# The first gates of a late block copied on the chip, and attention's background steps set by their count, in a hybrid decoder block

## The chip, the cores and the metric

The kernel runs on one core of a Trainium2 chip. The core has TensorE for matmuls (PE in the profile; PEld is its weight load), VectorE (DVE), ScalarE (ACT), GpSimd (POOL) and SyncE (SP). Each executes its own instructions in order, and they meet by semaphores. DMA transfers are issued here by SyncE (plain ones) and by GpSimd (gathers by a list of indices). The metric is the device time of one execution in microseconds (us), less is better.

## What is computed

The reference is one decoder layer on 1024 tokens of width 1024, in float32:

```python
h = rmsnorm(x, norm1_g) * (1 + sc1) + sh1
mq, mk, mv, mo, mi, mf, dq, dk, dv = split(h @ w_in)       # 4 mLSTM heads, 4 attention heads
hm = rmsnorm(mlstm_chunkwise(silu(conv(mq, mk)), mv, gates(mi, mf))) * sigmoid(mo)
od = rmsnorm(softmax(q1 k1) v - lam * softmax(q2 k2) v) * (1 - lam_init)   # causal, 2 maps a head
x = x + g1 * (concat(hm, od) @ w_out)
h2 = rmsnorm(x, norm2_g) * (1 + sc2) + sh2
x = x + g2 * peer(h2)
out = rmsnorm(x, final_g)
```

`peer` takes for each token and each of 8 heads the 16 best of 16384 experts (product keys, 128 x 128), so 128 experts a token. With gate g (a softmax over the 16) and expert rows u, v of length 1024 it sums g * gelu(h2 . u) * v.

## The kernel before, in words

The tokens are eight blocks of 128. They pass the **front** in three groups (`GROUPS`, 2, 3 and 3 blocks): `front_T` (norm and transpose), `front_proj` (seven projections, whose weights stream in 256 KB pieces `wr` through seven buffers on SyncE's queue), `front_mix` (what is left of attention and mLSTM, and their norms), `front_out`, `front_norm2` and `front_keys` (queries, keys, the search for the best experts).

The experts of blocks 0, 1, 6 and 7 are **gathered**: for each of the 128 places one gather of rows u (`gu`, 512 KB) that VectorE multiplies with h2, then one of rows v (`gv` or `gvr`) that is summed into `ga`. The experts of blocks 2 to 5 (`DENSE`) go by **dense** matmuls over all 16384 experts: for each of 128 keys j, `s_mm` makes `ge` = gelu(h2 . u), `s_gate` multiplies it by the gates `Gt` and splits it into W (two parts), and `v_step` multiplies W by the rows v into `ps_dA`. `s_mm` runs up to 14 keys ahead (`AHEAD`).

The gates of a dense block are made by `gates`: 32 steps, each of two VectorE operations (`oh`), eight matmuls (`ps_g`) and one ScalarE copy into `stg`. Four steps fill one `stg` (1 MB: all 128 keys of 16 tokens), which is then written to `G_d` in DRAM (32 writes for the four blocks). `load_G(j)` reads the gates of eight keys from there for all tokens (2 MB) into the one buffer `Gt`. Blocks 2 to 4 are handled in the front as a background stream (`all_gates`). Block 5 is the **late** block: it comes with the third group, and its gates are made inside `dense`, with buffers of `LateMem`, while the first `s_mm` run. So the first `Gt` is read in two loads: 1.5 MB for the three early blocks, and, when all late steps are through, 512 KB for the late one.

Work that runs beside the projections is kept in `background` as generators with a rate. `tick` adds the rate to each one's account and advances it once per whole unit. `proj_T` and `proj_R` call `tick` behind each piece of weights, `att_S` calls it for each part of scores, and `front_mix` between attention's steps. The rates: the gathers 1.6 (`RG`), the tables of gates 1.5 (`RP`), mLSTM 0.4 and 1.0, attention `AR[k]`. `attention` yields once for the first unit's scores and twice for each unit, a unit being one head of one block; `att_load` reads a head's `akT` and `avh` from DRAM. When the projections are over, `front_mix` takes the remaining streams of its group off the list and runs them out itself:

```python
k = 0
for _ in o.att[0]:
    k += 1
    if k % 2 or k % 4 == 0:
        next(steps, None)
        tick()
for _ in steps:
    pass
```

All this writes a program order. A planner then orders the instructions of every engine by that order (shifted by priorities: the late steps ahead, the gathers that are left over after the front behind it, and `dense` behind those) and by its own costs; the engines execute the result as it stands.

Of the kernel before, what the change touches and what calls it, by code (L numbers as in the profile page):

```python
# [15 lines left out]
AF = mybir.ActivationFunctionType  # L16
# [5 lines left out]
P = 128  # L22
# [6 lines left out]
HD = 4  # L29
# [22 lines left out]
def kernel(ctx: ExitStack, tc: tile.TileContext, x, c_col, ada_w, ada_b, ada_bc, n1c,  # L52
                             w_in, conv_w, conv_b, gate_b, mngc, lq1, lk1, lq2, lk2, dngc, w_out,
                             n2c, n2r, wq, skT, pu, puT, pv, fg, out, dbg=None):
    nc = tc.nc
# [4 lines left out]
    LPACE = ()  # L60
    PJ = 0
    ALT = 1
    AR = [0.6, 0.5, 0.3]
    SOG = [8, 0, 8]
    DEF = 0
    N1G = 2
# [28 lines left out]
    J, JG = 4, 8  # L95
# [233 lines left out]
    TS = 16  # L329
# [362 lines left out]
    def front_proj(o):  # L692

        n, nb, t0 = o.n, o.nb, o.t0
# [9 lines left out]
        nc.sync.dma_start(vd_d[t0 * P:t0 * P + n, :].rearrange("(b p) e -> p b e", p=P), vst[:, :nb])  # L704
        o.a_, o.b_ = mlstm_rows(o.hT, nb)
        o.mix = [fr.tile([P, D], F32, tag="rows", name="mix", bufs=RB) for _ in range(nb)]
        o.att = [attention(o), AR[o.k], 0.0]
        background.append(o.att)
        overlapped.append(o)
        o.qk = []  # L710
# [34 lines left out]
    def attention(o):  # L745

        units, o.ams = att_heads(o.t0, o.nb, o.dq, o.mix)
        att_S(units[0])
        yield
        for k, u in enumerate(units):  # L750
            if k + 1 < len(units):
                att_S(units[k + 1])
            yield
            att_T(u)
            att_V(u)
            yield
# [443 lines left out]
            nc.sync.dma_start(quarter(out, c), xo[c * 32:(c + 1) * 32])  # L1200

    class FrontMem:
        gs = staticmethod(lambda s, d: fr.tile(s, d, tag="gs", name="gs", bufs=1))
        gh = staticmethod(lambda s, d: fr.tile(s, d, tag="gh", name="gh", bufs=1))
        dT = staticmethod(lambda s, d: fr.tile(s, d, tag="dT", name="dT", bufs=DB))
        stg = staticmethod(lambda s, d: fr.tile(s, d, tag="stg", name="stg", bufs=SB))
# [4 lines left out]
    def gates(ii, gf, db, wide, mem=None):  # L1211
# [5 lines left out]
        mem = mem or FrontMem()  # L1217
# [20 lines left out]
        def close(oh, stg, tg, q):  # L1238
            pg = mem.bank("ps_g")
            for r in range(4):  # L1240
                for i in range(np_):
                    nc.tensor.matmul(pg[:, r * P:(r + 1) * P], oh[:, 0, :, r], oh[:, 2 + i, :, r],  # L1242
                                     start=i == 0, stop=i == np_ - 1)
            nc.scalar.activation(stg[:, :, q * 4:q * 4 + 4].rearrange("p j t -> p t j"),  # L1244
                                 pg.rearrange("p (t j) -> p t j", t=4), AF.Copy)
            if q == TS // 4 - 1:
                nc.sync.dma_start(G_d[db * (P // TS) + tg], stg)

        for tg in range(P // TS):
            stg = mem.stg([P, P, TS], F32)  # L1250
# [12 lines left out]
    @contextmanager  # L1263
    def later(offset):

        tc.cur_priority += offset
        yield
        tc.cur_priority -= offset


    def dense(d1, d2, d3, d4, psS, psA):
        n = NDB * P
        blocks = DENSE + MIXED
        na = len(blocks) * P
# [3 lines left out]
        Gt = {}  # L1278
        d1.tile([P, 72], F32, name="pad")

        def load_G(j, parts=((0, na // TS),)):
            if parts[0][0] == 0:
                Gt[0] = d1.tile([P, na // TS, JG, TS], F32, tag="G", name="Gt", bufs=GD)
            for lo, hi in parts:
                nc.sync.dma_start(Gt[0][:, lo:hi], G_d[lo:hi, :, j:j + JG, :].rearrange("a p j t -> p a j t"))

        class LateMem:
# [2 lines left out]
            gh = staticmethod(lambda s, d: d4.tile(s, d, tag="gh", name="gh", bufs=1))  # L1290
            dT = staticmethod(lambda s, d: d4.tile(s, d, tag="dT", name="dT", bufs=1))
            halves = []

            @staticmethod
            def stg(s, d):
# [10 lines left out]
        if gating:  # L1306
            early = gating[0][2] * P // TS
            load_G(0, ((0, early),))
            late = (s for g in gating for s in gates(*g, mem=LateMem))
        else:  # L1310
            load_G(0)
            acc = d4.tile([P, len(blocks), D], F32, tag="dacc", name="dacc", bufs=1)
# [115 lines left out]
        if gating:  # L1428
            with later(-LP):
                for _ in late:  # L1430
                    pass
            load_G(0, ((early, na // TS),))
            acc = d4.tile([P, len(blocks), D], F32, tag="dacc", name="dacc", bufs=1)
        for j in range(J):
            s_gate(j)
# [129 lines left out]
```

## Time and profile before

| what | us |
|---|---|
| median of 3 runs | 2989.22 |
| lowest and highest run | 2983.14, 2993.66 |
| the profiled execution | 2983.2 |
| its span in the profile | 2981.3 |
| TensorE busy | 2783.4 |
| VectorE busy | 2382.0 |
| GpSimd busy | 1282.8 |
| ScalarE busy | 973.6 |

The profile shows one execution. Its span runs from the first instruction to the last. "Busy" is the time in which an engine executed matmuls or other compute; the clock is the share of full speed that was granted to TensorE. A row of a group shows the count, the summed busy time in us, the mean of one in ns, and, behind the second bar, the idle time of the engine just ahead of these instructions with what ended it. `<-` reads "written from" or "waits for".

### The profile page before, as it was taken

Reading aid. Unit: us, or ns where it says so; the run is one execution under the profiler, and the core shown is the slowest. Engines: PE = TensorE matmul, PEld = TensorE weight load, DVE = VectorE, ACT = ScalarE, POOL = GpSimd, SP = SyncE. Lnnn points to the kernel's source line nnn. Section 1 sums busy time; section 2 is a strip of 40 time slices with the busy share of each in tenths; the row PEclk is TensorE's granted clock in tenths of the full one; section 3 lists DMA queues with packets and bytes.
Section 4 is the critical chain, followed back from the end, with each engine's and each line's share of the span. In section 5 each row is a group of like instructions: output and inputs, shape, how many; then the busy total and the mean of one; then the engine's idle time right before and its main releaser. Section 6 shows DMA issues by size and latency. Waiting matters only on the chain.

```text
span 2981.3 us, 40087 instructions
## 1 busy us (share of the span) xinstructions
PE 2783.4 (93%) x13686; PEld 2076.9 (70%) x13686; DVE 2382.0 (80%) x5489; ACT 973.6 (33%) x1695; POOL 1282.8 (43%) x1083
## 2 busy tenths in 40 slices
PE   6899999689999997999995999999999999999998
PEld 5547757465556765766574878878777788877786
DVE  5634999856997687357977988889988889988876
ACT  1432344312235445232453322322322323322232
POOL 0000266654555453334654555545554444544400
PEclk9989999689999999999997999999999999999999
DMA  8745699999998888998788999999899999999962
GB/s 280 252 138 180 209 360 336 324 350 339 325 345 306 305 299 293 350 332 293 280 309 284 337 335 334 332 340 340 313 339 322 331 341 324 338 323 317 318 230 70
DMA packets 396848, 900.00 MB, mean 302 GB/s; under 512 B 34770, under 2 KB 184274, under 8 KB 392548
## 3 DMA queue, kind: packets, MB, share of 16 engines
q0 software_dynamic: 147456, 536.94, 50.1%
q1 hardware_dynamic: 249188, 360.51, 35.9%
q8 instruction: 108, 1.77, 0.2%
q14 instruction: 96, 0.79, 0.1%
HBM read 846.97 MB, written 50.35 MB: 301 GB/s over the span
## 4 chain that ended last, share of the span: by engine, by line
PE 50%; DVE 18%; DMA 13%; issue 11%; POOL 5%; ACT 2%; SPq 0%; DVEq 0%; POOLq 0%; ACTq 0%
PE ps_pj L403 11%; PE ps_dS L1338 9%; PE ps_dA L1370 9%; DMA Gt<-G_d 8%; PE ps_pj L423 7%; DVE gu L1028 4%; PE ps_g L1242 3%; PE ga L1090 3%; POOL gvr L1057 3%; DVE ga L1064 2%; DMA gu<-in_peer_u_dram,ei 2%; PE ps_S L605 2%; DVE dvs L1364 1%; DMA gv<-in_peer_v_dram,eT 1%; PE ps_tr L379 1%
## 5 line engine op out<-in xcount | busy, mean ns | idle before, releaser
L1024 POOL DMA_INDIRECT gu<-in_peer_u_dram,ei x512 | 657.3, 1284 | 928.6 <-DVE sv L912 347.9
L1370 PE MATMUL ps_dA<-dvs,W 128*128 128x512 f32 x2976 | 720.8, 396 | 56.9 <-ACT W L1348 27.4
L1338 PE MATMUL ps_dS<-dhT,us 128*128 128x512 f32 x3072 | 731.0, 391 | 1.2 <-POOL us L1331 1.2
L1370 PEld LDWEIGHTS ps_dA<-dvs,W 128*128 128x128 f32 x2976 | 566.1, 191 | 188.9 <-ACT W L1348 27.4
L1028 DVE SCALAR_TENSOR_TENSOR gu<-gu,h2r 128x1024 f32<-128x1024 f32 x512 | 620.1, 1222 | 72.3 <-DMA gu<-in_peer_u_dram,ei 59.1
L1338 PEld LDWEIGHTS ps_dS<-dhT,us 128*128 128x128 f32 x3072 | 576.2, 188 | 129.4 <-issue 8.0
L1057 POOL DMA_INDIRECT gvr<-in_peer_v_dram,ei x256 | 301.5, 1178 | 339.0 <-DVE ga L1064 184.4
L1076 POOL DMA_INDIRECT gv<-in_peer_v_dram,eT x256 | 275.8, 1077 | 266.0 <-PE ga L1090 148.2
L1064 DVE SCALAR_TENSOR_TENSOR ga<-gvr,w,ga 128x1024 f32<-128x1024 f32 x254 | 326.9, 1287 | 1.7 <-issue 0.3
L1363 ACT ACTIVATE dvs<-dv 128x512 fp32r<-128x512 f32 x248 | 155.7, 628 | 368.4 <-PE ps_dA L1370 164.5
L403 PE MATMUL ps_pj<-hT,wr 128*128 128x384 f32 (+1 forms) x768 | 233.7, 459 | 3.1 <-ACT ae L598 2.9
L403 PE MATMUL ps_pj<-h2T,wr 128*128 128x384 f32 (+1 forms) x768 | 231.2, 454 | 0.0
L1339 ACT ACTIVATE ge<-ps_dS 128x512 f32<-128x512 f32 x128 | 76.5, 598 | 424.4 <-PE ps_dS L1338 413.3
L1244 ACT ACTIVATE stg<-ps_g 128x512 f32<-128x512 f32 x128 | 134.0, 1064 | 238.0 <-PE ps_g L1242 164.1
L403 PEld LDWEIGHTS ps_pj<-hT,wr 128*128 128x128 f32 x768 | 144.9, 193 | 79.5 <-issue 9.8
L1255 DVE TENSOR_TENSOR oh<-iotah,dT 128x1024 f16<-128x1024 f16 x128 | 102.2, 804 | 118.5 <-PE ps_g L1242 94.7
L403 PEld LDWEIGHTS ps_pj<-h2T,wr 128*128 128x128 f32 x768 | 142.2, 190 | 73.3 <-issue 9.9
L423 PE MATMUL ps_pj<-wr,hT 128*128 128x256 f32 (+1 forms) x672 | 182.1, 425 | 3.5 <-DMA wr<-in_w_in_dram 2.7
L1364 DVE TENSOR_TENSOR dvs<-dv,dvs 128x512 fp32r<-128x512 f32 x248 | 171.9, 698 | 16.4 <-ACT dvs L1363 16.4
L1347 DVE SCALAR_TENSOR_TENSOR ge<-ge,Gt 128x512 f32<-128x512 f32 x128 | 87.3, 692 | 119.1 <-DMA Gt<-G_d 112.9
L423 PEld LDWEIGHTS ps_pj<-wr,hT 128*128 128x128 f32 x672 | 128.5, 197 | 45.4 <-issue 23.8
L1377 DVE TENSOR_TENSOR dacc<-dacc,ps_dA 128x512 f32<-128x512 f32 x240 | 156.1, 683 | 4.6 <-PE ps_dA L1370 4.6
(294 smaller groups left out, 3333.1 us busy)
## 6 DMA issues: line engine op xcount, KB each, us to landing
u<-in_peer_uT_dram SPq DMA_DIRECT2D x128, 512.0 KB
dv<-in_peer_v_dram SPq DMA_DIRECT2D x248, 256.0 KB
wr<-in_w_in_dram SPq DMA_DIRECT2D x168, 256.0 KB
G_d<-stg SPq DMA_DIRECT2D x32, 1024.0 KB
Gt<-G_d SPq DMA_DIRECT2D x15, 2048.0 KB
wmod<-in_ada_w_dram SPq DMA_DIRECT2D x48, 512.0 KB
wr<-in_peer_w_query_dram SPq DMA_DIRECT2D x96, 256.0 KB
wr<-in_w_out_dram SPq DMA_DIRECT2D x48, 256.0 KB
```

The lines of the kernel that those rows point to most:

```text
L403: nc.tensor.matmul(out[f], w2[:, kh, f * P:(f + 1) * P], hT[:, kb, :n], start=kb == 0 and f % k == 0, stop=kb == NC - 1 and f % k == k - 1)
L423: nc.tensor.matmul(out[f], hT[:, kb, f * P:(f + 1) * P], wk[:, kh], start=kb == 0 and f % k == 0, stop=kb == NC - 1 and (f % k == k - 1 or ...
L1024: nc.gpsimd.indirect_dma_start(out=u, out_offset=None, in_=pu, in_offset=bass.IndirectOffsetOnAxis(ap=o.ei[:, k:k + 1], axis=0))
L1028: nc.vector.scalar_tensor_tensor(u, u, 1.0, o.h2, op0=OP.mult, op1=OP.mult, accum_out=o.z[:, k:k + 1])
L1057: nc.gpsimd.indirect_dma_start(out=vt, out_offset=None, in_=pv, in_offset=bass.IndirectOffsetOnAxis(ap=o.ei[:, k:k + 1], axis=0))
L1064: nc.vector.scalar_tensor_tensor(o.acc, vt, o.w[:, k:k + 1], o.acc, op0=OP.mult, op1=OP.add)
L1076: got = nc.gpsimd.indirect_dma_start(out=vt, out_offset=None, in_=pv, in_offset=bass.IndirectOffsetOnAxis(ap=o.eT[:, t:t + 1], axis=0))
L1338: nc.tensor.matmul(ps, us[:, a, c], hT[:, b, c, sl], start=c == 0 and i == 0, stop=c == NC - 1 and i == 2)
L1363: nc.scalar.activation(vs[:, 0], v, AF.Copy)
L1364: nc.vector.tensor_sub(vs[:, 1], v, vs[:, 0])
L1370: nc.tensor.matmul(pacc[tb], w[:, a, tb * P:(tb + 1) * P], vs[:, b], start=jj == 0 and i == 0, stop=jj == J - 1 and i == 2)
L1377: nc.vector.tensor_add(o, o, pacc[tb])
```

## The change

Two edits. In `gates`, the first eight keys of each late `stg` are copied by ScalarE into `Gt` right after the `stg` is issued for writing, and the 512 KB load of the late block's first gates is dropped; the write to `G_d` stays, for the other keys. And attention's rate is no longer taken from the list 0.6, 0.5, 0.3: it is the number of attention's steps over the 32 ticks that follow in the projections, that is 17/32 = 0.53 for two blocks and 25/32 = 0.78 for three.

```diff
-    AR = [0.6, 0.5, 0.3]
...
-        o.att = [attention(o), AR[o.k], 0.0]
+        o.att = [attention(o), (2 * HD * nb + 1) / 32.0, 0.0]
...
     class FrontMem:
+        first = None
...
             if q == TS // 4 - 1:
                 nc.sync.dma_start(G_d[db * (P // TS) + tg], stg)
+                if mem.first is not None:
+                    nc.scalar.activation(mem.first[:, db * (P // TS) + tg], stg[:, 0:JG], AF.Copy)
...
             halves = []
+            first = None
...
             load_G(0, ((0, early),))
+            LateMem.first = Gt[0]
             late = (s for g in gating for s in gates(*g, mem=LateMem))
...
                 for _ in late:
                     pass
-            load_G(0, ((early, na // TS),))
             acc = d4.tile([P, len(blocks), D], F32, tag="dacc", name="dacc", bufs=1)
```

## Rows read from the trace of the kernel before

**Rows 1.** The page: the span, and the gate products of the dense part.

```profile
span 2981.3 us, 40087 instructions
...
L1347 DVE SCALAR_TENSOR_TENSOR ge<-ge,Gt 128x512 f32<-128x512 f32 x128 | 87.3, 692 | 119.1 <-DMA Gt<-G_d 112.9
```

**Rows 2.** Stretches: busy us (instructions) of PE, PEld, DVE, ACT, POOL; clock, DMA share, GB/s.

```profile
196.70:209.50 12.80, 6.28 (x49) 5.42 (x47) 7.21 (x37) 7.25 (x22) 0.00 (x0) 0.91 0.46 156
387.00:536.00 149.00, 141.99 (x610) 98.94 (x609) 137.81 (x327) 68.20 (x157) 104.54 (x77) 0.95 0.96 343
536.00:598.50 62.50, 31.85 (x101) 18.74 (x99) 54.38 (x141) 19.36 (x55) 38.35 (x31) 0.57 0.93 322
853.00:1068.00 215.00, 212.32 (x1278) 146.33 (x1277) 165.84 (x375) 99.29 (x184) 113.60 (x91) 0.97 0.89 310
1068.00:1183.40 115.40, 92.88 (x648) 59.26 (x647) 93.60 (x221) 59.23 (x129) 49.96 (x43) 0.93 0.87 312
1188.00:1484.00 296.00, 287.13 (x1942) 191.41 (x1939) 197.60 (x796) 97.45 (x130) 138.57 (x119) 0.99 0.90 318
...
1583.30:1610.70 27.40, 0.05 (x2) 0.01 (x1) 15.70 (x27) 2.40 (x5) 14.06 (x12) 0.50 0.94 340
1610.70:2846.00 1235.30, 1207.89 (x5222) 989.30 (x5223) 1113.10 (x1524) 369.76 (x556) 613.46 (x494) 0.99 0.94 328
```

**Rows 3.** Waits, 1575 to 1660: waiter, releaser, us, times, longest.

```profile
PE ps_dA L1370 <- ACT W L1348: 27.4, 1, 27.4
```

**Rows 4.** The chain that ended last: start us, us, what.

```profile
1591.69 17.57 DMA Gt<-G_d
...
1614.22 12.56 DMA Gt<-G_d
...
1841.64 5.44 PE ps_dS L1338 x24
```

**Rows 5.** Timeline of ScalarE, 1579 to 1616: start us, us, what.

```profile
1581.10 1.06 ACT L1244 ACTIVATE stg<-ps_g 128x512 f32<-128x512 f32 x1
...
1610.01 3.64 ACT L1348 ACTIVATE W<-ge 128x512 fp32r<-128x512 f32 x6 [24.97 <-DVE ge L1347]
```

**Rows 6.** Timeline of ScalarE, 568 to 612.

```profile
600.65 0.28 ACT L1051 ACTIVATE wT<-ga 128x128 f32<-128x128 f32 x1 [2.88 <-DVE eT L1049]
```

**Rows 7.** Groups by line, TensorE, 536 to 598.5.

```profile
L605 PE MATMUL ps_S<-akT,dq 64*128 64x512 f32 (+2 forms) x24 | 15.1, 754 | 7.8 <-DMA akT<-kd_d 7.8
L638 PE MATMUL ps_o<-avh,aT 128*128 128x128 f32 x46 | 10.8, 401 | 2.9 <-ACT aT L631 2.3 <-issue 0.6
L629 PE MATMUL ps_at<-ident,ae 128*128 128x128 f32 x21 | 5.1, 395 | 16.0 <-DVE ae L618 16.0
```

**Rows 8.** Groups by line, VectorE, 536 to 598.5.

```profile
L1028 DVE SCALAR_TENSOR_TENSOR gu<-gu,h2r 128x1024 f32<-128x1024 f32 x33 | 39.6, 1219 | 5.2 <-DMA gu<-in_peer_u_dram,ei 3.5 <-issue 1.7
```

**Rows 9.** Groups by line, TensorE, 1068 to 1183.4.

```profile
L605 PE MATMUL ps_S<-akT,dq 64*128 64x512 f32 (+2 forms) x56 | 26.0, 575 | 1.6 <-ACT ajunk L642 0.8 <-issue 0.8
L1242 PE MATMUL ps_g<-oh 128*128 128x128 f16 x185 | 25.8, 295 | 12.1 <-ACT stg L1244 12.1
L638 PE MATMUL ps_o<-avh,aT 128*128 128x128 f32 x120 | 17.2, 298 | 2.0 <-ACT aT L631 1.1 <-issue 1.0
L1090 PE MATMUL ga<-gv,strip 128*32 128x256 f32 x208 | 16.7, 445 | 2.6 <-DMA gv<-in_peer_v_dram,eT 2.6
L629 PE MATMUL ps_at<-ident,ae 128*128 128x128 f32 x57 | 9.4, 293 | 4.2 <-ACT ae L598 1.7 <-ACT aT L631 1.1 <-issue 0.9
```

**Rows 10.** Stretches, gathers of rows u alone (line 1024): POOL, clock, DMA share, GB/s.

```profile
1583.00:2846.00 1263.00, 324.53 (x249) 0.97 0.94 329
```

**Rows 11.** Timeline of VectorE, 2866 to 2868: the last gathered block's result.

```profile
2866.65 1.29 DVE L1168 SCALAR_TENSOR_TENSOR fx<-fx,gms 128x1024 f32<-128x1024 f32 x1
```

**Rows 12.** Groups by line, ScalarE, 387 to 536.

```profile
L598 ACT ACT_TABLE_LOAD x5 | 6.4, 1283 | 4.3 <-DVE ast L595 4.2
```

**Rows 13.** Waits of TensorE, 387 to 536.

```profile
PE ps_pj L403 <- ACT ae L598: 2.9, 1, 2.9
```

## The prediction, made before the changed kernel was run

> **What bounds the kernel now.** I read the page first. The profiled execution took 2983.2 us and its span is 2981.3 us [rows 1]; this is 6 us under the median of the runs, 2989.2. Then I read the stretches of the span in one table [rows 2]. From 1610.7 on, the dense matmuls set the time: TensorE is busy 1207.9 of 1235.3 us. Ahead of that TensorE is again what is full, but not everywhere, and the change touches the three holes. First, 1583.3 to 1610.7: TensorE 0.05 us busy in 27.4. Second, 536 to 598.5, the rest of the second group's attention behind its projections: busy 31.85 of 62.5, at a mean granted clock of 0.57. Third, 1068 to 1183.4, the same rest in the third group: 92.88 of 115.4.
>
> The view of waits explains the first hole: the first matmul of the second dense product waits 27.4 us for W [rows 3], W for the gate product `ge`, and that for the load of `Gt`. In the chain this load takes 17.57 us from its issue at 1591.69 [rows 4]. It is the late block's 512 KB, and it could not be issued before the block's last `stg` had been written to `G_d`. That `stg` was complete on the chip at 1582.16 [rows 5], 28.5 us before the first matmul that needs it.
>
> **The change, part by part.** *The late block's gates.* Removed: one load of 512 KB and the write-then-read around it. Added: eight ScalarE copies of 128x128, one behind each fourth step. The nearest row, a 128x128 copy, took 0.28 us [rows 6], so 8 x 0.28 = 2.2 us, on an engine that is idle for half of that stretch; each stands in the chain of late steps, so without this cover the chain grows by the same 2.2 us. The wait for the write remains only in the load of keys 8 to 15, which still goes by `G_d`.
>
> What is late next? After the last `stg` (1582.16) come the copy, 0.3, the first gate product, 0.69 [rows 1], and W's high part, 0.61 [rows 5]: 1583.8. VectorE, in order, has other work standing there (gather products of 1.22 us, the finish of block 1), so I put the first matmul at 1584 to 1590 and not at 1610.7. Then eight keys are ready: two groups of 96 matmuls, and 24 run in 5.44 us [rows 4], so 43.5 us of TensorE work. In that time keys 8 to 15 must land: their load can go when eight products are done (5 us) and the last write is in, so at about 1593; before, it took 12.56 us [rows 4]. Even with 17.57 it is there at 1611, with work till 1630. So nothing takes the wait's place on TensorE: the gain is 27 at best, 18 if VectorE's queue holds it up. I take **24 us**: the load is gone, the queue is the only delay left.
>
> *The ticks.* Behind `o.att` a group makes 16 + 8 + 8 = 32 calls of `tick` in its projections. Attention has 2 x 4 x nb + 1 steps, 17 or 25. The old rates give it 19 steps (all 17 done), 16 of 25, and 9 of 25; with the new ones the 17th or 25th step falls on the 32nd tick. The first group only spreads. I cost that at nothing, since its last units' work already falls into the 12.8 us of its rest [rows 2]; two units later would add at most 2 x 4.0 us (a unit's wait, below). In the second group 9 steps move forward, in the third 16: by the trace four units' scores and seven. Their `akT` and `avh` loads move too, past weight loads on SyncE's queue: one pair in the second group, two in the third.
>
> What stays in the rest is `mlstm_out` and `mix_end`. The first group shows this case: 12.8 us from the last projection matmul to the first transpose of `mix`, with two blocks [rows 2]. With three that is 19; gather products share VectorE there, so I take 25 in the second group and 30 in the third.
>
> *Second group.* The rest shrinks from 62.5 to 25. TensorE's part of what moves is 15.1 + 10.8 + 5.1 = 31 us [rows 7], at 0.57 of the clock; in the projections, at 0.95, it is some 19. There TensorE has 149 - 142 = 7 us free and VectorE 11 [rows 2]. VectorE's part is at most 54.4 - 39.6 = 15 us, 39.6 being gather products [rows 8]. So the projections grow by 12 if gathers give way, and by 15/(1 - 0.63) - 11 = 29 if gathers keep their 77 x 1.22 = 94 of 149 us. I take 15: gathers have no due time here, and behind this stage VectorE is half free. Net -62.5 + 25 + 15 = **-22**, bounds -31 (19 and 12) and -4 (30 and 29).
>
> *Third group.* The rest shrinks from 115.4 to 30. Attention's TensorE work in it is 26.0 + 17.2 + 9.4 = 52.6 us [rows 9], and the projections have 2.7 us free. So they grow by 50; if gate steps and value rows keep the share they have in the rest and before it (25.8 + 16.7 of 115 us, 28% in the projections), by 69. Net -35 to -16. About a third of the net is background work that these us no longer hold; it comes back after 1188, where TensorE is 97% busy [rows 2]: 5 to 11 us. That leaves -30 to -5. I take **-15**, nearer the dear end, since TensorE is full on both sides.
>
> *Ticks lost.* `front_mix` ticks no more: 7 and 12 ticks less, at 1.6 gathers each 30 gathers. In the 1263 us from 1583 the last two blocks have 249 gathers of rows u [rows 10] and all 2 x 128 of rows v, so 2.50 us each, and the last result is done at 2868 [rows 11], 113 us ahead of the end. A front that is 37 us shorter holds some 16 gathers less (77 in 149 us, 91 in 215 [rows 2]), 40 us of the stream: covered.
>
> Sum: 2983.2 - 24 - 22 - 15 = 2922. Since the median of before is 6 us above its profiled execution, I add half of that: **2925**.
>
> Attention's Exp will stand among more Silu and Sigmoid evacuations; a load of ScalarE's tables takes 1.283 us, and Exp alone has five of them in the second group's projections [rows 12], where ScalarE is 68 of 149 us busy. I put this at nothing, with a rival below. The Trainium skill speaks against such mixing ("ScalarE: Activation LUTs", section "Table sets: the hidden batching unit"): activations should be batched by table set, since each change of set loads a table. The same page of the Trainium skill gives 2.66 us for a change with its drain; eleven moved units at two changes each would be 59 us by that estimate.
>
> **Rivals.** *Only the copy pays.* What moves costs in the projections what it saves behind them. For it: TensorE is 99% busy in the third group's projections. Against: the second group's hole is half idle and near half clock. 2983 - 24 + 3 = 2962.
> *Both rests go to their bounds.* -24 - 31 - 30 gives 2901; with the copy's best and no background coming back, 2890.
> *The copy's gain is eaten.* VectorE's queue or the next load takes the wait's place and 5 of 24 us remain; the finish of block 1 stands right there. 2944.
> *The gather stream ends last.* If the 30 gathers of the lost ticks and the 16 of the shorter front add up, 46 x 2.5 = 115 us, it ends at 2868 - 37 + 115 = 2946, behind the dense matmuls. It decides from about 36 deferred gathers on. Against: the stream ran behind its ticks already, so lost ticks should cost it little. 2948.
> *Table loads set evacuations back.* Eleven units at two loads of 1.283 us, all on the path: 28 us, 2953.
> *Slower.* TensorE, in order, stands in the projections for attention's softmax, as in the second group's rest: 16.0 us for VectorE's `ae` over four units [rows 7], 4.0 each. Eleven units move. For slower by 0.3% they must lose the 61 us and 9 to 12 more, 72/11 = 6.5 us each, with every projection matmul queued behind. Against: in the second group's projections of before, nine units cost TensorE one such wait of 2.9 us and little else [rows 13]. About 3000.
>
> **Chances.** Forecast, 2908 to 2942: 0.45. Only the copy: 0.19. Both bounds: 0.11. Copy eaten: 0.07. Gathers last: 0.07. Tables: 0.05. Slower: 0.06. The range of 2890 to 2972 leaves out the last and the far sides of the second and third. 0.3%, 9 us, is about what a measurement of this kernel can tell. Faster by more than that: all but the slower case and the upper end of "only the copy", 0.87; within it 0.07; slower 0.06.
>
> **What would show it.** Right: the first `ps_dA` matmul waits under 6 us; no 512 KB load of `Gt`; from the last `mo` matmul to the first transpose of `mix` 20 to 35 us in the second and third group; their projections longer by some 15 and 50 to 70; the dense part some 60 us earlier and as long as before; the last gather result at 2850 to 2890. Wrong: a wait for `Gt` or W that merely moves to key 8; TensorE idle in the projections behind `ae`; a rest that stays long because gather products or gate steps fill VectorE; gathers at the very end.

## The result: slower, and the profile after

The changed kernel takes 3031.0 us, median of 5 runs (3023.1 to 3033.4), beside 2990.8 us for the kernel before in the same measurement: ratio 1.0132, 95% interval 1.0112 to 1.0152. The forecast was 2925 us with a range of 2890 to 2972. The profiled execution took 3030.4 us and its span is 3028.6, so the span grew by 47.3 us.

The table gives the marks by which the two traces are compared (in both, from the views of the tiles `akT`, `mo` and `mix` and of the second dense product). A stage here runs from a group's first `akT` load to the first transpose of its `mix`.

| us | before | after | change |
|---|---|---|---|
| first group's first transpose of `mix` | 209.5 | 205.8 | -3.7 |
| second stage: projections to the last `mo` | 161.4 | 227.9 | +66.5 |
| second stage: the rest | 62.7 | 22.3 | -40.4 |
| between second and third stage | 251.1 | 260.7 | +9.6 |
| third stage: projections | 217.4 | 323.8 | +106.4 |
| third stage: the rest | 114.5 | 16.5 | -98.0 |
| on to the first matmul of the second dense product | 429.1 | 412.1 | -17.0 |
| from there to the end | 1370.6 | 1394.4 | +23.8 |

The stretches of the profile after, for the two stages (projections, rest, projections, rest), the piece between the last `stg` and the dense matmuls, and the dense part. Columns as in [rows 2]:

```profile
370.90:598.80 227.90, 191.52 (x735) 126.81 (x733) 198.73 (x452) 79.83 (x198) 156.21 (x114) 0.84 0.93 331
598.80:621.10 22.30, 8.62 (x56) 5.41 (x56) 17.44 (x62) 7.04 (x19) 12.13 (x11) 0.66 0.67 230
...
881.80:1205.60 323.80, 304.28 (x1825) 199.79 (x1824) 240.24 (x524) 150.55 (x297) 149.55 (x134) 0.93 0.87 306
1205.60:1222.10 16.50, 9.59 (x86) 7.51 (x85) 12.22 (x47) 9.98 (x19) 2.33 (x3) 0.81 0.85 270
...
1627.70:1634.20 6.50, 1.93 (x16) 0.68 (x16) 2.52 (x5) 1.96 (x5) 2.36 (x3) 0.50 1.04 415
1634.20:2904.00 1269.80, 1225.72 (x5361) 1002.03 (x5362) 1117.46 (x1535) 374.89 (x563) 621.35 (x498) 0.98 0.93 325
```

Both rests shrank as forecast, and both projections grew by as much or more. In the second group's projections TensorE was 95% busy at a granted clock of 0.95 [rows 2]; now it is 84% busy, at 0.84. Its waits in that stage, the longest seven sums (waiter, releaser, us, times, longest), answer to [rows 7, 13]:

```profile
PE ps_o L637 <- DMA avh<-vd_d: 12.3, 2, 10.7
PE ps_S L604 <- DMA akT<-kd_d: 10.7, 2, 7.3
PE ga L1089 <- DMA gv<-in_peer_v_dram,eT: 9.4, 1, 9.4
PE ps_o L637 <- ACT aT L630: 5.6, 7, 1.8
PE ps_S L604 <- ACT ae L597: 4.4, 1, 4.4
PE ps_at L628 <- DVE ae L617: 4.3, 2, 2.9
PE ps_up L529 <- ACT kw L524: 1.5, 3, 0.8
```

Before, TensorE's one long wait for a head's load stood in the rest (7.8 us for `akT`); now it meets four such waits, 23.0 us, with projection matmuls queued behind. The wait for the softmax (`ae` by VectorE, 16.0 us in the rest before) is down to 4.3. The 9.4 us for `gv`, gathered rows v, stand in the rest, and the kernel before has no such wait there. Over the whole stage TensorE is 200.1 of 250.2 us busy, and was 186.4 of 224.1, so of 26 us some 14 are busy time and 12 idle; the mean clock of the whole stage is 0.82 and was 0.85, since the old rest stood at 0.57.

The copy works as described. ScalarE's timeline after (start us, us, what) answers to [rows 5]: the last `stg`, the last of eight copies at 0.31 us, and W 4.5 us behind it, where there were 25 us before.

```profile
1626.80 1.90 ACT L1244 ACTIVATE stg<-ps_g 128x512 f32<-128x512 f32 x2
1628.73 0.31 ACT L1249 ACTIVATE Gt<-stg 128x128 f32<-128x128 f32 x1
1633.55 3.66 ACT L1352 ACTIVATE W<-ge 128x512 fp32r<-128x512 f32 x6 [4.51 <-DVE ge L1351]
```

The waits of TensorE in the dense part, and the span of the matmuls that sum gathered rows v of blocks 0 and 1 (the tile's view: ns least, median, most; first and last start):

```profile
PE ps_dA L1374 <- DVE dvs L1368: 36.0, 13, 9.4
...
PE ps_dA L1374 <- ACT W L1352: 2.4, 1, 2.4
```

```profile
L1089 PE MATMUL ga<-gv,strip x2048: 376/379/637, 608.0 to 1692.8; 128*32 128x256 f32 x187
```

The W that was 27.4 us late [rows 3] is 2.4 us late. But the last rows v are summed at 1692.8, 59 us into the dense part; before, the last were summed at 1559.0, ahead of it.

### The profile page after: what moved, and what is told of

Same layout as the page of the kernel before. It is cut to its first block, busy times and chain, and to the rows that moved or that the text cites. A ratio compares the mean times of both kernels' runs of the same rounds, so it can differ in the third digit from the quotient of the medians.

```text
span 3028.6 us, 40065 instructions
## 1 busy us (share of the span) xinstructions
PE 2806.1 (93%) x13686; PEld 2086.9 (69%) x13686; DVE 2387.9 (79%) x5489; ACT 978.2 (32%) x1707; POOL 1281.5 (42%) x1083
## 4 chain that ended last, share of the span: by engine, by line
PE 43%; DVE 23%; DMA 18%; issue 11%; POOL 3%; ACT 2%; SPq 0%; DVEq 0%; POOLq 0%; ACTq 0%
PE ps_pj L402 11%; PE ps_pj L422 8%; DMA Gt<-G_d 7%; DVE gu L1027 5%; PE ps_dS L1342 5%; PE ps_dA L1374 5%; DVE ga L1063 4%; DMA gu<-in_peer_u_dram,ei 4%; PE ps_g L1242 3%; PE ga L1089 3%; DVE dvs L1368 2%; DVE dacc L1381 2%; POOL gvr L1056 2%; PE ps_S L604 2%; DMA wmod<-in_ada_w_dram 2%
## 5 line engine op out<-in xcount | busy, mean ns | idle before, releaser
L402 PE MATMUL ps_pj<-hT,wr 128*128 128x384 f32 (+1 forms) x768 | 244.1, 475 | 2.1 <-ACT ae L597 2.1
L1089 PE MATMUL ga<-gv,strip 128*32 128x256 f32 x2048 | 155.1, 405 | 26.1 <-DMA gv<-in_peer_v_dram,eT 24.2
L1242 PE MATMUL ps_g<-oh 128*128 128x128 f16 x1024 | 139.6, 296 | 26.2 <-ACT stg L1244 16.4
```

The source lines that it names most:

```text
L402: nc.tensor.matmul(out[f], w2[:, kh, f * P:(f + 1) * P], hT[:, kb, :n], start=kb == 0 and f % k == 0, stop=kb == NC - 1 and f % k == k - 1)
L1089: mm = nc.tensor.matmul(o.acc[c * 32:(c + 1) * 32, q * QW:(q + 1) * QW], st[:, q, 31 + 32 * i - r:63 + 32 * i - r], vt[:, c * QW:(c + 1) * ...
```

## The experiments

Eighteen kernels ran. The kernel before stood at 2983.2 to 2992.0 us beside them, so rows are best compared by their ratios. A stage or a dense part is that of one profiled execution; kernels whose second group has the same rate, loads and length of products agree in the second stage within 5 us (221.0 to 224.1 with the old rates, 245.4 to 250.2 spread). "Copy" is the late block's copy, "old rates" are `AR` = 0.6, 0.5, 0.3. Single times are marked "1". Rows v in the dense part are its `ga` matmuls divided by 8 (2048 matmuls sum 256 gathered rows).

| run | us | ratio, 95% | 2nd stage | 3rd stage | dense part | rows v in it |
|---|---|---|---|---|---|---|
| before | 2990.8 | | 224.1 | 331.9 | 1370.6 | 0 |
| after | 3031.0 | 1.0132 (1.0112, 1.0152) | 250.2 | 340.3 | 1394.4 | 10 |
| e1 copy only | 2973.5 | 0.9953 (0.9934, 0.9972) | 222.7 | 333.1 | 1380.6 | 0 |
| e2 spread only | 3037.1 | 1.0170 (1.0143, 1.0196) | 248.4 | 336.9 | 1387.9 | 6 |
| e3 copy, second group spread | 3003.2 | 1.0055 (1.0034, 1.0076) | 249.9 | 322.1 | 1377.0 | 2 |
| e4 copy, third group spread | 2998.8 | 1.0033 (1.0018, 1.0048) | 221.6 | 355.5 | 1372.5 | 0 |
| e5 after, one head's loads | 3018.9 | 1.0104 (1.0082, 1.0126) | 238.7 | 346.8 | 1395.0 | 12 |
| e6 copy, one head's loads | 2993.6 | 1.0032 (1.0016, 1.0048) | 234.2 | 337.9 | 1370.7 | 0 |
| e7 after, half the gathers | 3029.2 | 1.0147 (1.0121, 1.0173) | 245.4 | 344.9 | 1449.2 | 68 |
| e8 after, ticks kept | 3017.7 | 1.0106 (1.0083, 1.0130) | 247.2 | 366.9 | 1374.5 | 0 |
| e9 after, gathers held | 3086.4 (1) | | 248.2 | 334.4 | 1505.1 | 122 |
| e10 copy, gathers held | 3079.0 (1) | | 222.7 | 316.7 | 1507.2 | 120 |
| e11 as e4, no inner ticks | 3016.0 | 1.0103 (1.0075, 1.0131) | 221.0 | 343.0 | 1442.3 | 74 |
| e12 copy, slower rates | 2989.4 | 1.0003 (0.9988, 1.0018) | 239.9 | 350.8 | 1372.3 | 0 |
| e13 after, short products | 2976.8 (1) | | 233.1 | 310.1 | 1385.1 | 12 |
| e14 copy, short products | 2949.6 (1) | | 201.0 | 303.4 | 1387.4 | 2 |
| e15 as e13, one head's loads | 2961.8 (1) | | 202.7 | 304.2 | 1413.8 | 22 |
| e16 as e14, one head's loads | 2956.5 (1) | | 194.1 | 299.7 | 1404.9 | 10 |
| e18 after, heads ahead | 3004.9 | 1.0058 (1.0035, 1.0080) | 232.0 | 325.3 | 1399.6 | 14 |
| e19 copy, heads ahead | 2971.9 | 0.9949 (0.9931, 0.9968) | 227.0 | 323.3 | 1380.4 | 0 |

**The change in its parts (e1 to e4).** e1, e3 and e4 are the changed kernel with another rate in one line; e2 is the kernel before with the first of these lines in the place of its own rates.

```diff
-        o.att = [attention(o), (2 * HD * nb + 1) / 32.0, 0.0]
+        o.att = [attention(o), (0.6, 0.5, 0.3)[o.k], 0.0]       # e1
+        o.att = [attention(o), (0.6, 25 / 32, 0.3)[o.k], 0.0]   # e3
+        o.att = [attention(o), (0.6, 0.5, 25 / 32)[o.k], 0.0]   # e4
```

> The copy alone; attention keeps its old rates. Theory A (the spreading costs about 50 us ahead of the dense part, and the work that it puts off eats the copy's gain of 23.5 us there): with the spreading gone the gain stays, 2991 - 23.5 = 2967 us (2964 to 2975). Theory B (the dense part takes the copy's gain back whatever stands ahead of it, since the loads of the gates for keys 8, 16 and 24 and the split of the values set its pace): 2980 to 2991. Theory C (the copy itself costs more than the load that it replaces): over 2994.

> The spreading alone; the late block's gates still come by the 512 KB load. Theory A: the work put off would be done while TensorE waits for the load, so the copy is worth little beside the spreading and the time is 3031 to 3043 us. Theory B: the same, 3031 to 3041. If copy and spreading simply add up: 3031 + 23.5 = 3054 (3048 to 3060), and the spreading's own price is 50 us ahead of the dense part and more behind it. A rival that puts the loss on the copy: 2970 to 2995.

> The copy, and the new rate in the second group alone (25 steps in 32 ticks in place of 16). Theory A: the second group's part of the loss is the 27 us seen between its two marks, so the copy-only time plus 22 to 30 us. Theory of a ripple (the second group only moves work that the third would have done anyhow): within 8 us of the copy alone. Forecast of the prediction's own step for this group: 22 us below the copy alone.

> The copy, and the new rate in the third group alone (25 steps in 32 ticks in place of 9). Theory A: the third group's own loss is about 22 us at its first transpose of the mixed rows, and some 15 us more behind it from the gathers of block 1 that are put off into the dense part: the copy-only time plus 25 to 40 us. If the third group only suffers from what the second puts off: within 8 us of the copy alone. Forecast of the prediction's own step for this group: 15 us below the copy alone.

The copy alone gains: 2973.5 us, inside the range of theory A (2964 to 2975) at its upper end. Spreading alone loses 48 us. On top of the copy, the second group's spreading costs 30 us (3003.2 - 2973.5), the third's 25 (2998.8 - 2973.5), and both 57 (3031.0 - 2973.5; 54 by the ratios): they add up. The third does not merely suffer from the second. The copy is worth 16 us alone (2989.3 measured for before beside it) and 6 beside the spreading (3037.1 - 3031.0; 11 by the ratios), so a part of A holds too: the spreading takes some of the copy's gain.

By the marks, the profile after is 58.5 us longer than e1's: 27.5 in the second stage, 7.3 between the stages, 7.2 in the third, 7.1 from there to the second dense product, 13.7 in the dense part, less 4.4 ahead of the second stage. So the second stage is about half of the loss.

In e1 the copy's place shows its full worth. The stretches of e1 for the second stage (projections, rest), from the last `stg` to the dense matmuls, and the dense part:

```profile
375.30:537.10 161.80, 155.00 (x653) 107.06 (x653) 148.54 (x346) 68.92 (x160) 111.26 (x81) 0.95 0.95 343
537.10:598.00 60.90, 29.60 (x102) 18.22 (x100) 54.97 (x141) 19.43 (x56) 35.72 (x32) 0.59 0.92 330
...
1583.40:1589.50 6.10, 0.04 (x1) 0.04 (x1) 4.95 (x5) 5.64 (x9) 4.25 (x3) 0.68 0.78 258
1589.50:2970.10 1380.60, 1331.27 (x5760) 1089.91 (x5760) 1219.91 (x1687) 408.94 (x628) 631.21 (x505) 0.98 0.89 312
```

The first matmul of the second dense product stands at 1589.5, and from there to the end it takes 1380.6 us, 10.0 more than before, with the same 5760 TensorE instructions. VectorE's share there is 12.6 us larger than before's 1207.3. That gather products which ran in the 27.4 us hole [rows 2] now run beside dense matmuls fits it, but e12 has 1372.3 with nearly as many products, so this is argued and not shown.

**The heads' loads, first try (e5, e6).**

```diff
-        if u.first:
+        if u.first and u.h == 0:
             att_load(u)
...
-            if w.h == u.h:
-                w.kT, w.vh = kT, vh
+            w.kT, w.vh = kT, vh
```

> The changed kernel, but in each group the first head's keys and values serve all four heads: the loads of heads 2 to 4 are left out, all arithmetic stays. Theory A1 (in the second group TensorE, in order, stands in the projections for the heads' loads, 10.7 + 12.3 us for akT and avh, because one head's buffers must come free first): the second group's first transpose of mix moves from 621 to about 600, and the end by 15 to 30 us, 3000 to 3016. Theory A2 (the waits for loads only stand in front of waits for the softmax chain and for VectorE, which come out instead): 3022 to 3033.

> The copy with the old rates, and the same three loads of each group left out. Theory A1 (the loads are dear only where the even spacing brings them into the projections): 2 to 8 us under the copy alone, 2965 to 2972, TensorE's wait for akT in its second group being 8.4 us. If the loads cost any schedule the same: as far under the copy alone as the run beside it is under the changed kernel, 15 to 30 us.

Neither came out as expected. With spreading, the end moved by some 8 us only (ratio 1.0104 against 1.0132) and the second stage from 250 to 239; the waits of TensorE there became these:

```profile
PE ps_S L603 <- ACT ae L596: 13.0, 3, 7.5
PE ps_up L529 <- DVE num L516: 6.6, 1, 6.6
PE ps_o L636 <- ACT aT L629: 6.5, 9, 1.6
PE ps_at L627 <- DVE ae L616: 4.4, 2, 2.9
```

The loads' 23 us went and waits for the exponentials came up. So A2 looks half right. With the old rates the second stage got 12 us longer without the loads, and the whole kernel 24 us slower by the ratios; a wait of 12.2 us for VectorE (`ps_at` for `ast`) stands in that stage which e1 doesn't have, but why is not known. Yet the difference between spread and old rates in that stage fell from 27.5 us (250.2 - 222.7) to 4.5 (238.7 - 234.2). That needed a cleaner test.

**Gathers and ticks (e7 to e11).** In e7 the gathers' rate is halved in the second group's projections; in e8 the lost ticks are given back; in e9 and e10 the gathers are put on the list of background steps only after the second group's `front_mix`; in e11 the scores make no ticks of their own in the third group's projections:

```diff
+        if o.k == 1:                                   # e7, back to RG behind the projections
+            flow[1] = RG / 2
...
+        for _ in range((0, 7, 12)[o.k]):               # e8, at the end of front_mix
+            tick()
...
-                    background.append([streams[0], RG, 0.0])   # e9, e10: moved here
         front_mix(o)
+        if k == 1:
+            background.append([streams[0], RG, 0.0])
...
-                tick()                                 # e11, in att_S
+                if not quiet:
+                    tick()
```

> The changed kernel with 0.8 in place of 1.6 gathers a tick in the second group's projections; no work is left out, the gathers come later. Theory A3 (attention's chain is stretched there by the gathers: their products on VectorE, 1.22 us each, and their transfers beside the heads' loads): the second group's first transpose of mix 15 to 30 us earlier than 621, and the end 0 to 20 us earlier, since some of the gathers come back later. Theory A1 with loads that wait only for buffers: that transpose moves less than 8 us, and the end is the same or later.

> The changed kernel, with the 7 and 12 ticks that the mixing of the second and third group lost given back at its end. Theory D (the lost ticks put gathers off into the dense part, which took back 23.5 us of the copy's gain): the dense part 10 to 20 us shorter, the end 3012 to 3024. If lost ticks are covered, as the prediction had it: 3028 to 3040, the ticks only lengthening the two rests.

> The changed kernel with all gathers held back until the second group's attention is over; no work is left out. What counts is the second stage, from its first akT load to its first transpose of mix: 250 us in the changed kernel, 223 in the copy alone. Theory A3 (VectorE's queue, which holds about 130 gather products of 1.22 us in that stage, stretches each hand-over of the softmax, and TensorE, in order, stands behind it in the projections): 185 to 205 us here, and no longer than the run beside it with the old rates. Theory A1 (loads and the chain itself, whatever VectorE does): 225 to 245 us here, and longer than the run beside it. The whole time goes up in both, since some 130 gathers go behind the stage at up to 2.5 us each: 3050 to 3300.

> The copy with the old rates, and the gathers held back in the same way. Second stage, 223 us in the copy alone: theory A3: 190 to 210 us, the rest behind the projections down from 60 to some 35 us and the spread kernel beside it as short or shorter. Theory A1: 200 to 215 us and 20 us or more shorter than the spread kernel beside it.

> The copy with the new rate in the third group alone, but the scores of attention make no ticks of their own while they stand in that group's projections; the work that these ticks issue comes later. Theory E (the moved units bring gate steps and value rows with them by their own ticks, which is why the projections grew by 116 us and not by 50 to 69): the third stage, from its first akT load to its first transpose of mix, 355 us with these ticks, comes down to 300 to 330, and the end stays within 10 us of 2999, since the work is only moved. Theory F (it is the granted clock and waits of the chain): the stage stays over 345 us.

The three edits of gathers did not do what they were for. Even in e9 the second stage holds as many gather products as the changed kernel's, 120, here from the groups by line of VectorE, 373 to 621:

```profile
L1027 DVE SCALAR_TENSOR_TENSOR gu<-gu,h2r 128x1024 f32<-128x1024 f32 x120 | 144.7, 1216 | 17.4 <-DMA gu<-in_peer_u_dram,ei 17.2
```

A tick sets the place of a gather in the program's written order; the planner then orders the instructions by its own costs, and here the gathers stand in the stage again. So e7, e9 and e10 say nothing on the second stage, and A3 was still open.

They do show what deferred work costs in the dense part. The dense part lengthens with the rows v of block 1 that are put off into it: 68 rows in e7, 120 in e10, 122 in e9 and 74 in e11 go with 1449.2, 1507.2, 1505.1 and 1442.3 us. Against 1375 us, about the middle of the runs without such rows (1370.6 to 1380.6), that is 1.1, 1.1, 1.1 and 0.9 us a row. By this the changed kernel's 10 rows make some 10 of its 24 us. It is not what they cost in all, since the front gets shorter where rows leave it: e7's second dense product starts 60 us earlier than the changed kernel's (1573.8 and 1634.2), its dense part is 55 us longer, and its ratio is the same within the noise. With few rows the relation is loose (25 us over 1375 with 14 rows in e18, 12 with 2 in e14), so other work stands there too. In e8, where the ticks are kept, no row is left and the dense part is back at 1374.5; its third stage is 27 us longer, and by the ratios some 8 us are won. Theory D holds in the dense part, but 12 of the 20 us that it gains there are paid in front (the second dense product starts at 1646.5). In e11 the third stage came down from 355.5 to 343.0 only, over the bound of E (330) and just under that of F (345); the gate steps and rows v that came with the moved units' own ticks are a part of its growth, not the whole, and put off they cost more: e11 ends 21 us behind e4 by the ratios.

**Slower rates (e12).** `(0.6, 0.4, 0.2)[o.k]` in place of the old rates.

> The copy, with attention slower than before in the second and third group's projections: 0.4 and 0.2 steps a tick in place of 0.5 and 0.3. If every unit that leaves the projections gains what one that came in cost (25 to 30 us for 9 and for 16 steps, so 2 to 3 us a step, with 3 and 3 steps): 2973 - 12 to 18 = 2955 to 2961. If the old rates stand near the best: 2970 to 2985.

A miss: 2989.4 us, 16 behind the copy alone. Units that leave the projections don't give back what those that enter them cost; both stages got longer (239.9 and 350.8). Of the rates tried, the old ones are the best.

**Loads and products parted (e13 to e16).** The product of a gathered row with 64 columns in place of 1024 for blocks 0 and 1, without and with the edit of e5:

```diff
+            m = 64 if o.tb < 2 else D
-            nc.vector.scalar_tensor_tensor(u, u, 1.0, o.h2, op0=OP.mult, op1=OP.mult, accum_out=o.z[:, k:k + 1])
+            nc.vector.scalar_tensor_tensor(u[:, :m], u[:, :m], 1.0, o.h2[:, :m], op0=OP.mult, op1=OP.mult, accum_out=o.z[:, k:k + 1])
```

> The changed kernel, with the products of the gathered u rows of blocks 0 and 1 cut from 1024 to 64 columns (15 of 16 parts of these dot products are left out; their transfers stay). The second stage, from its first akT load to its first transpose of mix, is 250 us in the changed kernel. Theory A3 (the softmax's hand-overs wait in VectorE's queue behind these products, some 120 x 1.22 = 146 us in the stage): 185 to 215 us, and no longer than with the old rates beside it. Theory A1 (loads and the unit's own chain): 230 to 250 us, and still 20 us or more longer than with the old rates.

> The copy with the old rates and the same short products; second stage 223 us in the copy alone. Theory A3: 190 to 215 us, with the rest behind the projections down from 60 to 30 to 45 us. Theory A1: 210 to 223 us.

> The changed kernel with the short products and with one head's keys and values for all four heads (both parts left out as in the runs of one of them). Second stage: if products and loads are the two causes of the longer projections, 175 to 200 us, and at or under the run beside it with the old rates. If the chain of a unit (scores, exponentials, transposes, values) is itself too long for 32 ticks: 215 us or more, and over the run beside it.

> The copy with the old rates, the short products and one head's keys and values. Second stage: 185 to 210 us if products and loads set it; 210 to 223 us if the unit's own chain does.

The second stage, in us, spread less old rates:

| | all loads | one head's loads |
|---|---|---|
| products of 1024 | 250.2 - 222.7 = 27.5 | 238.7 - 234.2 = 4.5 |
| products of 64 | 233.1 - 201.0 = 32.1 | 202.7 - 194.1 = 8.6 |

The rows of this table decide for the second stage. Shorter products make every entry shorter, by 17 to 40 us, but at either rate: VectorE's queue is a price of the stage, and not of the spreading there (A3 falls, 233 where at most 215 was expected). Without the loads the penalty of spreading is nearly gone, with either length of product (A1). In e13, where VectorE's busy time is halved, TensorE waits 13.6 us for `akT` and 13.2 for `avh` all the same; e14 waits 9.5 for both. e15, 202.7 us, lies just over the range of "products and loads" and far under that of the unit's own chain.

The whole times say something else: spread less old rates is 57 us with all loads and long products, 25 with one head's loads (e5, e6), 27 with short products (e13, e14) and 5 with both (e15, e16; single runs). So outside the second stage the products seem to have a part in the loss, as far as single runs can tell.

**Loads a head ahead (e18, e19).** Nothing is left out here: four buffers for `akT` and `avh`, the next head's loads issued at a head's first unit; five weight buffers in place of seven and six work buffers (`t2`) in place of eight make room.

```diff
-        if u.first:
-            att_load(u)
...
         units, o.ams = att_heads(o.t0, o.nb, o.dq, o.mix)
+        att_load(units[0])
         att_S(units[0])
         yield
         for k, u in enumerate(units):
+            if u.first and u.h + 1 < HD:
+                att_load(units[k + o.nb])
```

> The changed kernel with four buffers for heads' keys and values in place of two, each head's loads issued a head ahead; room for them comes from five weight buffers in place of seven and six small work buffers in place of eight. Nothing is left out. Theory A1: TensorE's waits for akT and avh in the second stage, 10.7 and 12.3 us, fall under 5 together, and the second stage comes within 12 us of the same edit at the old rates. If the loads were only one face of a slow chain: waits for the softmax take their place and the second stage stays 20 us or more above the old rates. The whole time, against 3031: 3010 to 3025 by the first, 3026 to 3045 by the second, since fewer weight buffers can only cost.

> The copy with the old rates, with the same buffers and loads a head ahead. Theory A1: the whole time lies 5 to 30 us under the spread kernel beside it, and the second stage 0 to 12 us under. Against the copy alone, 2973: 2965 to 2985, TensorE's one wait of 8.4 us for akT in its second stage gone, and fewer weight buffers to pay.

With early loads the spread kernel is some 22 us faster by the ratios (1.0058 against 1.0132), more than either theory gave it, and the second stage differs from the old rates by 5.0 us (232.0 and 227.0). TensorE's waits in it, in e18:

```profile
PE ga L1044 <- DVE w L1036: 12.7, 1, 12.7
PE ps_o L635 <- DMA avh<-vd_d: 7.1, 1, 7.1
PE ps_o L635 <- ACT aT L628: 7.0, 9, 2.1
PE ps_S L602 <- ACT ae L595: 6.1, 1, 6.1
```

One wait for a load is left, 7.1 us, where 5 was the bound. The two stages of e18 and then of e19:

```profile
371.30:603.30 232.00, 193.25 (x759) 131.38 (x757) 204.53 (x489) 86.84 (x214) 146.78 (x113) 0.83 0.92 327
867.00:1192.30 325.30, 303.62 (x1863) 201.83 (x1861) 244.90 (x560) 155.03 (x308) 153.63 (x134) 0.95 0.86 311
```

```profile
375.00:602.00 227.00, 185.59 (x758) 125.97 (x756) 202.89 (x486) 86.53 (x212) 145.28 (x113) 0.83 0.93 328
859.40:1182.70 323.30, 303.88 (x1899) 204.03 (x1899) 254.21 (x575) 157.50 (x309) 160.64 (x135) 0.96 0.89 312
```

The stages are now alike, and still e18 ends 33 us behind e19 (3004.9 and 2971.9). By the marks of the profiled executions (37.7 us apart) nearly all of it lies behind the stages: 15 us more in the late block's steps (183 us from the first dense product to the second's first matmul, against 168) and 19 us in the dense part, where 14 rows v stand. So the spreading has a second price behind the stages. In the dense part rows v are put off; that the longer late steps are work put off as well is argued and not shown. e19 and e1 are the versions that beat both kernels; between them there is no difference that these runs can tell. Early loads together with kept ticks were not tried.

## Why the prediction was wrong, step by step

*The copy* was right at its place: from the end of the last `stg` to the first matmul it was 28.5 us and is 5.5 (5.1 in e1), a gain of 23 for the 24 forecast; eight copies of 0.3 us took 2.4 us for 2.2; no 512 KB load is left. That this gain reaches the end was the weaker half: e1 keeps 16 us by the medians. The rival "the copy's gain is eaten" had the direction: some 8 us are lost where it had 19, and the cause stays open.

*The second group's step failed, and with it the sign.* The rest came to 22.3 us (25 forecast). The growth of the projections was put at 15, at most 29, and is 66.5. Two assumptions of that step failed. The first: the moved `akT` and `avh` loads were named, and costed at nothing. One head's two tiles fill the two buffers, so the next head's `akT` can be issued only when the scores of the head before are done, two steps of attention earlier. At 0.5 steps a tick that is 4 ticks, at 25/32 it is 2.6; a tick took 161.4/32 = 5.0 us, so by this estimate the even spacing cuts the lead from 20 us to 13. The traces show more. In both kernels each later `akT` is issued within 0.1 us of the end of the scores that free its buffer. The third head's load is an example (SyncE's issue, then TensorE; before, then after):

```profile
470.15 0.34 SPq L572 DMA_DIRECT2D akT<-kd_d  x1
...
471.96 8.68 PE L423 MATMUL ps_pj<-wr,hT 128*128 128x256 f32 x28 [0.88 <-ACT ae L598]
...
489.46 0.91 PE L605 MATMUL ps_S<-akT,dq 64*128 64x384 f32 x2
```

```profile
478.83 0.80 SPq L571 DMA_DIRECT2D akT<-kd_d  x1
...
480.04 1.16 PE L637 MATMUL ps_o<-avh,aT 128*128 128x128 f32 x8 [0.69 <-ACT aT L630]
488.48 1.62 PE L604 MATMUL ps_S<-akT,dq 64*128 64x384 f32 x2 [7.28 <-DMA akT<-kd_d]
```

Before, 48 projection matmuls and more stood between issue and use, 19.3 us, and TensorE did not wait for the load; after, no projection matmul stands there, and 7.3 of 9.7 us are a wait. The second head's load had 17.6 us before and 7.2 after, 3.4 of them a wait. TensorE stands for the load with every projection matmul behind it, and the granted clock is 0.84 over the projections, where it was 0.96. e5 with e6, e15 with e16, and e18 with e19 show it: without most of those waits, 5 to 9 us of 27 to 32 are left of the penalty. One thing goes along in two of these pairs: the changed kernel's stage holds four gathered rows v with 9.4 us of wait for them, which e5 and e18 don't have. In e13 TensorE has no such wait, and its penalty falls from 32.1 to 8.6 all the same.

The second assumption: gathers were to give way. They don't. Their products ran at 82 in 161.4 us before and at 114 in 227.9 us after, one in 2.0 us both times; counted to the first transpose, about 114 run in this stage at the old rates and 120 at the new. VectorE is 91% busy over the stage in e1 (148.5 + 55.0 of 222.7), so the rest of 62.5 us was not idle time to be had, and with three of four heads' loads left out the spread stage is still not shorter than the old one (4.5 to 8.6 us longer). The step also left out the DMA column of the rows that it read: 0.96 in the projections and 0.93 in the rest [rows 2]. A load that moves there meets transfers that nearly fill the DMA engines; how much of its time that costs, no run parts.

*The third group's step failed likewise.* The rest came to 16.5 us (30 forecast), the projections grew by 106 and not by 50 to 69. The trace said beforehand that TensorE was busy 92.9 of the rest's 115.4 us [rows 2]; the step moved attention's 52.6 us alone, and at its dear end added 19 us of the gate steps and value rows of longer projections; those of the rest itself stayed behind in it. They moved as well: e1's and e4's stages hold nearly the same TensorE instructions (1929 and 1922), at a granted clock of 0.94 and 0.88, and are 310.4 and 324.8 us busy. That the units' scores tick on their own account, and so bring gate steps and gathers along, was overlooked; e11 shows that as a part. Most of the 22 us by which e4's stage is longer is thus TensorE at lower clock (14 us) and the remainder idle time (8 us). No wait for a head's load shows in this stage, yet with early loads the penalty is 2.0 us, and why is open. The trace shows where e4 loses its time. From 895 to 1011, where e4 and then e1 stand at nearly the same place, it executes 147 matmuls less, at a clock of 0.76:

```profile
895.00:1011.00 116.00, 103.59 (x516) 59.70 (x515) 81.36 (x180) 49.15 (x95) 52.96 (x47) 0.76 0.82 288
```

```profile
895.00:1011.00 116.00, 115.02 (x663) 75.93 (x662) 85.75 (x195) 53.82 (x100) 60.06 (x48) 0.97 0.86 308
```

There TensorE meets ten waits of up to 2.1 us for the moved units' chain and the gate steps (`ae` 3.7 us, `stg` 3.4, `aT` 2.1, `qk` 2.1), where e1 has 0.2 for `ae` and none of the others. The low clock goes with these short waits; no run tests it alone.

*The lost ticks* were called hidden behind the gather stream's slack at the end. That slack was there: the last gathered result is at 2928.8, 100 us ahead of the end. It came 39 us later than the latest that was forecast (2890), but still ahead of the end. The price lies elsewhere, in rows v of block 1 that enter the dense part; giving the ticks back (e8) wins some 8 us in all.

*The rivals.* "Slower" was half right: TensorE, in order, stands in the projections, and the loss is some 30 us more than it said; it was put at 0.06. It looked at the softmax and weighed it by the nine units of before [rows 13], which had four ticks of lead; it should have looked at what those units had that the moved ones would lose. In the second group the longest waits are for loads; short waits for the softmax are seen in the third. "Only the copy pays" let the moved units cost what they save; they cost 26 us more in the second stage and 8 in the third. "Table loads" fell: ScalarE's table loads of 1.283 us are 13 in the second group's projections of before and 14 after, and 61 and 65 in the whole program, some 5 us more of an engine that is a third busy. What the Trainium skill says of mixed table sets ("ScalarE: Activation LUTs", section "Table sets: the hidden batching unit") therefore has little part in this difference; the projections mixed Exp with Silu and Sigmoid already.

## What to carry to other kernels

Before moving background work forward to fill a hole, write down for each load that moves how long before its use its buffer comes free, in ticks of the new spacing; an even spacing takes from each load the lead that an uneven one gave it, and an in-order engine makes everything behind it pay. Look at all engines of a "hole" over the whole stage: where VectorE is 91% busy, the DMA engines' share is 0.93, or TensorE is busy 92.9 of 115 us, moving work has little to win. And check in the trace that an edit of the written order moved what it names, since a scheduler may put the same instructions back.

## What the runs showed of the hardware that was not expected

- Four waits for loads of up to 10.7 us, and some smaller ones, go with a mean granted clock of 0.84 in 228 us, where it was 0.96. In e3 such waits end at 434.2 and 465.1; the stretches around them (ten us each; columns as in [rows 2]) show the clock at 0.50, and at 0.97 to 1.00 in the ten us after that:

```profile
430.00:440.00 10.00, 6.53 (x14) 3.07 (x13) 10.00 (x22) 4.29 (x10) 6.13 (x6) 0.50 1.01 387
440.00:450.00 10.00, 10.00 (x37) 6.06 (x36) 9.11 (x21) 3.29 (x7) 8.17 (x7) 1.00 0.85 279
...
460.00:470.00 10.00, 4.90 (x12) 3.42 (x13) 10.00 (x22) 4.74 (x10) 7.39 (x6) 0.50 0.91 328
470.00:480.00 10.00, 10.00 (x29) 5.01 (x29) 9.35 (x20) 2.06 (x5) 7.66 (x7) 0.97 0.92 326
```

  TensorE's wait was paid twice, once idle and once at the lower of its two levels: right behind the second wait eight projection matmuls took 4.82 us, ten us later eleven took 3.81. In the whole stage little of this is new, 0.82 against 0.85, since the rest of before was as slow.
- A gathered row's eight matmuls occupy TensorE for some 0.54 us in the dense part (36.4 us for 544 in e7), but each row put off into it lengthened that part by 0.9 to 1.1 us.
- Taking loads out made a stage longer (e6, 234.2 for 222.7 us), and so did both a faster and a slower rate (250 and 240 for 223): the length of this stage answers to small shifts of order by some 10 us, so a single neighbour is a poor control for an edit of that size.
